# Hybrid RWKV-7 / short-convolution block: the bonus row sums taken by float32 strips and spread by a load, and three kinds of stores requested by GpSimd

## The chip, the cores and the metric

The kernel runs on one core of a Trainium2 chip. The metric is the device time of one execution in microseconds (us). Three executions of the kernel before took 988.72, 988.27 and 989.01 us, median 988.72. The engines are named as in the profile: PE multiplies matrices (PEld is its weight load), DVE is the vector engine, ACT the scalar engine, POOL is GpSimd, and SP requests most of the transfers (DMAs).

## What is computed

One layer. A normalised input of 528 tokens (16 meta tokens and 512 real ones) by 2048 features is multiplied by one large matrix; half of its columns feed 16 recurrent heads of 64 channels, the other half a short convolution; both are gated, joined and multiplied by an output matrix. The change touches the bonus term of the recurrent heads, a sum over the 64 channels of a head, and the gate.

```python
P = hn @ w_in[l]
...
r, k, v, g_r = ...          # 1024 columns each, after the token shift
...
y = _rwkv7_recurrence(rh, decay, kh, vh, kk, kk * ah)
...
bonus = jnp.sum(rh * kh * r_k[l], axis=-1, keepdims=True) * vh
y_a = (yn + bonus.reshape(bsz, L, D_RWKV)) * jax.nn.silu(g_r)
...
mix = jnp.concatenate([y_a, y_b], axis=-1)
h_res = h_res + mix @ w_out[l]
```

## The kernel before

**Tiling.** Channels lie on the 128 partitions and tokens along the free axis. The recurrent heads are worked in 8 pairs, each 128 channels. The input product is a list of column tiles (lora, then k, r, v for the pairs, g for two pairs at a time, and the convolution's C, h, B and gc). A tile is 96 matmuls in two banks, or 48 in one, in four quarters of the contraction. Each weight is kept in two parts: `wr` holds 128x1024 raw float32 values, loaded by SP (line 159, three buffers); for each half, ACT makes the high part (line 151) and DVE the low part (line 152) in a `w` tile (six buffers). The products of a tile go to `ps_k`, `ps_C` and so on (lines 353 and 368).

**Two streams in one.** The function `mains` is a generator of those tiles. `prepare(i)` writes out the work of pair i and calls `fill(ns)` in between, which issues main matmuls worth that many nanoseconds by a counter kept in the program. `later(ns, fn)` puts an action off until that counter has gone on by ns. PE's instructions stand in the order in which they are written; those of the other engines are placed by a scheduler, and each engine works through its own list in order. `tc.issue_after(...)` keeps an instruction behind a named one.

**The pair's work.** `r` (128x512) is multiplied by the per-channel factor and by the key (line 735). In `gram_meta` a pair's squared keys `sq` are summed over each head's 64 channels by four float32 matmuls with a 128x32 block of `cs` (line 788, `key_norms`), each with 144 of the tokens and each writing another strip of 32 partitions of a bank that the next main tile is to use; ACT copies the sums to `n2`. For the bonus, `r` is split into a high and a low part (`rk_h` by ACT, line 665; `rk_l` by DVE, line 666), and two matmuls with a 128x128 block matrix `ones` (lines 820 and 821) write each head's sum into all 64 rows of the other head, in the bank `zb`; ACT copies that over `r` (line 822), DVE multiplies by `v` (line 920, called r times v here), and SP stores the product to `rbd[i]` for the end of the kernel. The value tiles are laid out with the heads swapped, which is why a head's sum goes to the other head's rows. After that come 16x16 triangular inverses on 72 partitions: a chain of small DVE operations (`prod`, `tt`, `y`, lines 874 to 889), which starts when the norms `nd` and blocks `d` have come back from memory.

**Single buffers.** `v` and `g` have one buffer each: the next `v` tile waits until r times v is done, and the second `g` of two waits until the first has been stored to `gated[i]` (line 473). The gate is formed by `g<-pr_g` (line 432) and `g<-th_r,g` (line 442) on DVE. Evacuations of C and h are `u<-ps_C` and `hh<-ps_h` (line 404), with a few columns mended by POOL from `ex` (line 407).

Of the kernel before, what the change touches and what calls it, by code (L numbers as in the profile page):

```python
# [9 lines left out]
F32 = mybir.dt.float32  # L10
F32R = mybir.dt.float32r
I32 = mybir.dt.int32
AF = mybir.ActivationFunctionType
ALU = mybir.AluOpType
# [4 lines left out]
P = 128  # L19
DM = 2048  # L20
KT = DM // P
SEQ = 512
META = 16
L = SEQ + META
CH = 64
NCH = SEQ // CH + 1
LP = NCH * CH
# [5 lines left out]
C_ID, C_GM, C_BM, C_ON = 0, 128, 384, 512  # L33
# [9 lines left out]
FW = dict(  # L43
    evac=34, start=1062, lora=2200, gram=8800, meta={0: 2000}, gram_b=13500, gram2=5500, misc=2000, v=2000, vt=1000, solve=24500, more={0: 5500, 2: 2400},
    tr=3200, lev=3000, cp=4200, out=1500, begin=19500, p=2900, u=2900, s=4200, mid=1000, last=3700, mix=2600,
)
# [43 lines left out]
def hymba_kernel(ctx: ExitStack, tc: tile.TileContext, xt, xtok, front, w_in, w_out, pv, lup, cst, msk, gf, out):  # L90
    nc = tc.nc
    ctx.enter_context(tc.manual_schedule(engines={mybir.EngineType.PE}))
    cp = ctx.enter_context(tc.tile_pool(name="cp", bufs=1))
    dp = ctx.enter_context(tc.tile_pool(name="dp", bufs=2, space=DRAM))
# [3 lines left out]
    cs = cp.tile([P, C_N], F32, name="cs")  # L98
# [6 lines left out]
    rbd = [dp.tile([P, SEQ], F32, tag=f"rbd{j}", name=f"rbd{j}", bufs=1) for j in range(NPAIR)]  # L105
    gated = [dp.tile([P, SEQ], F32, tag=f"gated{j}", name=f"gated{j}", bufs=1) for j in range(NPAIR)]
# [26 lines left out]
    quarters, chain, low = {}, {}, {}  # L133
# [35 lines left out]
    xp = ph1.enter_context(tc.tile_pool(name="xp", bufs=1))  # L169
# [3 lines left out]
    rst = xp.tile([P, 4], F32, name="rst")  # L173
    rsx = cq.tile([P, 2 * META], F32, name="rsx")
    la = cq.tile([P, 2, L], F32R, name="la")
    ones = xp.tile([P, P], F32R, name="ones")
    omm = xp.tile([P, 33], F32, name="omm")
    hv = xp.tile([P, 6, 8], F32, name="hv")
    hl = cp.tile([P, 2, 8], F32, name="hl")
# [3 lines left out]
    pi = ph1.enter_context(tc.tile_pool(name="pi", bufs=1, space=PSUM))  # L183
# [5 lines left out]
    def tr(name, dt=F32):  # L189
        return cq.tile([P, LP], dt, tag="tr", name=name, bufs=5)  # L190
# [122 lines left out]
    with tc.issue_after(head):  # L313
        nc.vector.tensor_scalar(
            out=omm, in0=pvt[:, V_MU : V_MU + 33], scalar1=-1.0, scalar2=1.0, op0=ALU.mult, op1=ALU.add
        )
        for d, off in (
# [4 lines left out]
                out=d, in0=pvt[:, off : off + 8], scalar1=0.5, scalar2=None, op0=ALU.mult  # L322
# [2 lines left out]
            out=hv[:, 4], in0=pvt[:, V_KA : V_KA + 8], scalar1=-0.5, scalar2=1.0, op0=ALU.mult, op1=ALU.add  # L325
        )

    nc.scalar.copy(ones, cs[:, C_BM : C_BM + P])
    FULL = ((0, 272), (272, L))
    TAIL = ((14, 272), (272, L))  # L330
    REAL = ((META, L),)
# [128 lines left out]
    def use(what, i, ps):  # L460
        if what == "lora":
            use_lora(ps)
        elif what in ("k", "v"):
            t = cq.tile([P, LP], F32, tag=what, name=f"{what}{i}")
            nc.gpsimd.memset(t[:, META:CH], 0.0)
            shift_full(ps, tile_of[what] + i, f"{what}{i}", padded(t))
            got[what, i] = t
        elif what in ("r", "g"):
            t = cq.tile([P, SEQ], F32, tag=f"r{i % 2}" if what == "r" else "g", name=f"{what}{i}")
            shift_real(ps, tile_of[what] + i, f"{what}{i}", t)  # L470
            if what == "g":
                gate(t, f"r{i}")
                later(14000, lambda: nc.sync.dma_start(gated[i], t))
            got[what, i] = t
        elif what == "C":
            u = tm(f"u{i}")
            scaled(TAIL, ps, u, 14)
            got[what, i] = u
        elif what == "h":
            u = got["C", i]  # L480
            hh = tm(f"hh{i}")
            with behind_of("turned"):
                scaled(TAIL, ps, hh, 14)
            n = SEQ + 2
            nc.gpsimd.tensor_tensor(out=u[:, 0:n], in0=u[:, 0:n], in1=hh[:, 0:n], op=ALU.mult)
            cv = tp.tile([P, SEQ], F32, tag="cw", name=f"cv{i}")
            nc.scalar.activation(cv, u[:, 0:SEQ], AF.Copy, scale=col(V_CW, i))
            for j in (1, 2):
                with behind_of("conv"):
                    nc.vector.scalar_tensor_tensor(  # L490
                        out=cv, in0=u[:, j : j + SEQ], scalar=col(V_CW, 8 * j + i), in1=cv, op0=ALU.mult, op1=ALU.add
                    )
            got[what, i] = cv
            if i == 0:
                nc.gpsimd.tensor_tensor(out=cv, in0=cv, in1=got["B", 0], op=ALU.mult)
        elif what == "B":
            b = tm(f"b{i}")[:, 0:SEQ] if i else tp.tile([P, SEQ], F32, name="b0")
            scaled(REAL, ps, b, META)
            got[what, i] = b
            if i:  # L500
                nc.gpsimd.tensor_tensor(out=got["h", i], in0=got["h", i], in1=b, op=ALU.mult)
        else:
            cv = got["h", i]
            g = tm(f"gc{i}")[:, 0:SEQ]
            with behind_of("split"):
                scaled(REAL, ps, g, META)
            gate(g, f"c{i}")
            o = direct.get(8 + i, cv)
            nc.vector.scalar_tensor_tensor(out=o, in0=cv, scalar=0.5, in1=g, op0=ALU.mult, op1=ALU.mult)
            if o is cv:  # L510
                later(9000, lambda: nc.sync.dma_start(mixd[8 + i], cv))
        ready.add((what, i))

    ready = set()
# [81 lines left out]
    def later(ns, fn):  # L596
        pending.append((clock[0] + ns, fn))
        pending.sort(key=lambda e: e[0])
# [16 lines left out]
    def fill(ns):  # L615
        while ns > 0:
            seen = len(ready)
            t = step()
            if t is None:
                return  # L620
            ns -= t
            if len(ready) > seen:
                ns += FW["evac"]
# [35 lines left out]
        nc.vector.tensor_tensor(out=lo, in0=raw, in1=hi.bitcast(F32), op=ALU.subtract)  # L659
        return hi, lo  # L660

    def split(t, name, n):
        hi = tr(f"{name}_h", F32R)[:, 0:n]
        lo = tr(f"{name}_l", F32R)[:, 0:n]
        nc.scalar.copy(hi, t)
        nc.vector.tensor_tensor(out=lo, in0=t, in1=hi.bitcast(F32), op=ALU.subtract)
        return hi, lo

    heads = [(h, slice(64 * h, 64 * h + 64), slice(64 - 64 * h, 128 - 64 * h)) for h in range(2)]

    place = [(i % 2) * 4 + i // 2 for i in range(NPAIR)]
# [11 lines left out]
    def behind(dst, src):  # L683
        with tc.issue_after(state["dma"]):
            nc.sync.dma_start(dst, src)
# [8 lines left out]
    def prepare(i):  # L694
        p = i % 2
# [35 lines left out]
        r = got["r", i]  # L731
# [6 lines left out]

        sq = tr(f"sq{i}")
        nc.scalar.activation(sq, k, AF.Square, scale=col(V_KK, i))  # L740
        rh, rl = split(r, f"rk{i}", SEQ)
        fill(FW["gram_b" if p else "gram"] + FW["meta"].get(i, 0))

        late = state["step"] > 48
# [16 lines left out]

        def gram_meta():
            z = early or next_banks()
            norms = key_norms(z[0][:, 96 : 96 + NS]) if late else None
            for h, hs, ho in heads:
                nc.tensor.matmul(
                    z[h][:, 0:META],
                    bk[hs, 0, h : h + 2, :].rearrange("p a s -> p (a s)"),
                    ar[hs, 0, 0, 0:META],
                    start=True, stop=True,  # L770
                )
            norms = norms if late else key_norms(z[0][:, 96 : 96 + NS])
            if p and "levels" in state:
                state["out"] = state.pop("levels").pop(0)(second_level(z))
            with ahead():
                for h in range(2):
                    nc.vector.tensor_tensor(
                        out=gt[:, h, 0, 0:META], in0=z[h][:, 0:META], in1=gmask[:, h, 0:META], op=ALU.mult
                    )
            with ahead():  # L780
                nc.scalar.copy(n2, norms)
            if "out" in state:
                state.pop("out")()
            state["banks"] = z

        def key_norms(z):
            for j in range(4):
                nc.tensor.matmul(
                    z[32 * j : 32 * j + 32], cs[:, C_BM + 48 : C_BM + 80], sq[:, j * NS : (j + 1) * NS],
                    start=True, stop=True, tile_position=(0, 32 * j),  # L790
                )
            return z
# [11 lines left out]

        NS = LP // 4
        n2 = tr(f"n2{i}")[:, 0:NS]
        if late:
            gram_meta()
        za = [pz.tile([P, 4, P], F32, tag="tz", name=f"g{i}_1_{h}") for h in range(2)]
# [4 lines left out]
            gram_meta()  # L814
        masked(za, 1, 5)
        masked(zc, 5, 9)
        fill(FW["gram2"] - FW["meta"].get(i, 0))

        zb = pi.tile([P, SEQ], F32, tag="ser", name=f"zb{i}")
        nc.tensor.matmul(zb, ones[:, 0:P], rh, start=True, stop=False)  # L820
        nc.tensor.matmul(zb, ones[:, 0:P], rl, start=False, stop=True)
        nc.scalar.copy(r, zb)
        fill(FW["misc"])


        bt = cq.tile([P, 2, NCH - 1, CH], F32, tag="bt", name=f"bt{i}")
        for a in range(2):
# [23 lines left out]
        nd = cq.tile([NB, 16], F32, tag="nd", name=f"nd{i}")  # L851
        behind(d, blocks(sg))
        behind(nd, sn.rearrange("(p s) -> p s", s=16))
        y = cq.tile([NB, 256], F32, tag="y", name=f"y{i}").rearrange("p (s t) -> p s t", t=16)
        nc.gpsimd.memset(y, 0.0)
        nc.vector.tensor_scalar(out=nd, in0=nd, scalar1=1e-24, scalar2=None, op0=ALU.max)
# [60 lines left out]
                    ))  # L917
        until("v", i)
        v = got["v", i]
        nc.vector.tensor_tensor(out=r, in0=r, in1=v[:, CH:LP], op=ALU.mult)  # L920
        later(12500, lambda: nc.sync.dma_start(rbd[i], r))
        fill(FW["v"])

        vs = cq.tile([P, NCH, CH], F32, tag="vs", name=f"vs{i}")
# [793 lines left out]
```

## Time and profile before

| | |
|---|---|
| time of three executions | 988.72, 988.27, 989.01 us |
| the profiled execution | 987.58 us, of which its span 985.8 us |
| granted PE clock, mean over the span | 0.998 |
| idle time of ACT before line 665, waiting for line 735 | 14.2 us, 7 times |
| POOL waiting to clear the next v, for r times v | 45.8 us, 7 times |
| SP waiting for a raw weight buffer (line 159, on line 152) | 239.9 us, 60 times |
| data moved | 174.74 MB, 213864 packets |

The span runs from the first to the last instruction; the time of an execution has 1.8 us more around it. A row of a wait names the waiting engine and line, what it waited for, the sum, the number of times and the longest.

### The profile page before, as it was taken

To read this page: it belongs to the slowest core of one execution; us is meant where nothing else is said; L and a number is where in the kernel's file an instruction comes from. 1 tells how busy PE (TensorE), PEld (TensorE's weight loads), DVE (VectorE), ACT (ScalarE), POOL (GpSimd) and SP (SyncE) were. 2 spreads that over 40 slices of the span, in tenths; PEclk is the share of its full clock that TensorE was granted. 3 is DMA by queue.
4 is the path that set the end of the run, shared out by engine and by line. 5 is a ranking of instruction groups with operands and counts; after the bars stand their busy time and mean duration, and the time that the engine had idled before them with its cause. 6 is when DMAs were issued, how large, how long until landed. Compare 5 with 4: busy or idle time off the path is not lost.

```text
span 985.8 us, 22369 instructions
## 1 busy us (share of the span) xinstructions
PE 976.5 (99%) x8999; PEld 906.3 (92%) x8999; DVE 708.3 (72%) x1423; ACT 401.0 (41%) x746; POOL 122.5 (12%) x241
## 2 busy tenths in 40 slices
PE   9999999999999999999999999999999999999996
PEld 9999999999998999998999998989899898888885
DVE  6787956578675678664678665455655799997897
ACT  7653323344322434322533322333343426556454
POOL 0120201112010111010110010010212102001001
PEclk9999999999999999999999999999999999999999
DMA  9526677256576285863285865997876799797654
GB/s 316 169 89 149 147 190 182 81 137 154 133 172 182 91 189 125 201 162 98 87 186 126 194 164 169 281 260 183 232 199 167 199 275 255 190 322 177 158 127 171
DMA packets 213864, 174.74 MB, mean 177 GB/s; under 512 B 157120, under 2 KB 177408, under 8 KB 213376
## 3 DMA queue, kind: packets, MB, share of 16 engines
q1 hardware_dynamic: 211312, 164.66, 61.2%
q0 software_dynamic: 2304, 8.39, 4.9%
q8 instruction: 70, 1.15, 0.5%
q14 instruction: 34, 0.28, 0.1%
q10 hardware_dynamic: 144, 0.26, 0.1%
HBM read 136.92 MB, written 36.35 MB: 176 GB/s over the span
## 4 chain that ended last, share of the span: by engine, by line
PE 93%; DVE 4%; issue 1%; DMA 1%; ACT 0%; POOL 0%; POOLq 0%; DVEq 0%; ACTq 0%
PE ps_v L353 9%; PE ps_C L353 9%; PE ps_g L353 9%; PE ps_gc L368 9%; PE ps_B L368 9%; PE ps_k L353 8%; PE ps_h L353 8%; PE ps_r L353 8%; PE M L1409 7%; PE P L1409 3%; PE g L755 2%; PE Q L1409 1%; PE ps_k L368 1%; PE ps_r L368 1%; PE ps_lora L368 1%
## 5 line engine op out<-in xcount | busy, mean ns | idle before, releaser
L152 DVE TENSOR_TENSOR w<-wr,w 128x512 fp32r<-128x512 f32 x252 | 174.9, 707 | 109.9 <-ACT w L151 104.0
L151 ACT CAST w<-wr 128x512 fp32r<-128x512 f32 x252 | 153.1, 619 | 246.9 <-PE ps_k L353 39.0
L353 PE MATMUL ps_v<-xh,w 128*128 128x256 f32 (+2 forms) x512 | 84.0, 284 | 0.0
L368 PE MATMUL ps_B<-xh,w 128*128 128x512 f32 x256 | 83.4, 394 | 0.3 <-DVE w L152 0.3
L353 PE MATMUL ps_h<-xh,w 128*128 128x256 f32 (+2 forms) x512 | 81.7, 281 | 0.0
L353 PE MATMUL ps_g<-xh,w 128*128 128x256 f32 (+2 forms) x512 | 81.4, 281 | 0.0
L368 PE MATMUL ps_gc<-xh,w 128*128 128x512 f32 x256 | 81.0, 392 | 0.0
L353 PE MATMUL ps_C<-xh,w 128*128 128x256 f32 (+2 forms) x512 | 80.8, 281 | 0.0
L353 PEld LDWEIGHTS ps_v<-xh,w 128*128 128x128 f32 x512 | 73.9, 188 | 0.3
L353 PE MATMUL ps_k<-xh,w 128*128 128x256 f32 (+1 forms) x448 | 73.3, 285 | 0.0
L353 PE MATMUL ps_r<-xh,w 128*128 128x256 f32 (+1 forms) x448 | 72.6, 281 | 0.0
L353 PEld LDWEIGHTS ps_g<-xh,w 128*128 128x128 f32 x512 | 71.9, 189 | 0.6 <-issue 0.2
L353 PEld LDWEIGHTS ps_h<-xh,w 128*128 128x128 f32 x512 | 72.1, 189 | 0.3
L353 PEld LDWEIGHTS ps_C<-xh,w 128*128 128x128 f32 x512 | 71.7, 189 | 0.2
L353 PEld LDWEIGHTS ps_k<-xh,w 128*128 128x128 f32 x448 | 64.7, 188 | 0.4
L353 PEld LDWEIGHTS ps_r<-xh,w 128*128 128x128 f32 x448 | 63.5, 189 | 0.4 <-issue 0.2
L368 PEld LDWEIGHTS ps_B<-xh,w 128*128 128x128 f32 x256 | 47.8, 188 | 10.3 <-DVE w L152 0.7
L368 PEld LDWEIGHTS ps_gc<-xh,w 128*128 128x128 f32 x256 | 47.7, 188 | 10.1
L353 PE MATMUL ps_h<-xl,w 128*128 128x256 f32 x256 | 56.7, 280 | 0.0
L353 PE MATMUL ps_C<-xl,w 128*128 128x256 f32 x256 | 55.9, 279 | 0.0
L353 PE MATMUL ps_v<-xl,w 128*128 128x256 f32 x256 | 55.8, 278 | 0.0
L353 PE MATMUL ps_g<-xl,w 128*128 128x256 f32 x256 | 55.4, 278 | 0.0
(384 smaller groups left out, 2085.2 us busy)
## 6 DMA issues: line engine op xcount, KB each, us to landing
wr<-in_w_in_dram SPq DMA_DIRECT2D x126, 512.0 KB
ct<-opd SPq DMA_DIRECT2D x72, 192.0 KB
wo<-in_w_out_dram SPq DMA_DIRECT2D x24, 512.0 KB
x<-in_w_out_dram POOLq DMA_DIRECT2D x16, 512.0 KB, 5.6
opd<-gt SPq DMA_DIRECT2D x16, 288.0 KB
bd<-bt SPq DMA_DIRECT2D x64, 64.0 KB
bw<-bd SPq DMA_DIRECT2D x16, 256.0 KB
x<-in_w_out_dram SPq DMA_DIRECT2D x8, 512.0 KB
```

Of the source, the lines that this page charges most:

```text
L151: nc.scalar.copy(hi, rq)
L152: low[q] = eng.tensor_tensor(out=lo, in0=rq, in1=hi.bitcast(F32), op=ALU.subtract).ins
L353: nc.tensor.matmul(ps[r][:, 0 : b - a], ww[:, k * P : (k + 1) * P], xx[:, kt, a:b], start=(kt == 0 and n == 0), stop=(kt == KT - 1 and n = ...
L368: nc.tensor.matmul(ps[r], ww[:, w], xx[:, kt, a:b], start=(kt == 0 and n == 0), stop=(kt == KT - 1 and n == 2))
L755: nc.tensor.matmul(z[h][:, c - c0], bk[hs, c, h : h + 2, :].rearrange("p a s -> p (a s)"), ar[hs, c].rearrange("p a s -> p (a s)"), start= ...
L1409: nc.tensor.matmul(bank[s], left(prod, jj, m, s), w, start=(jj == 0 and n == 0), stop=(jj == 7 and n == 2))
```

## The change

The bonus sums are now taken in `gram_meta`, beside the key norms and in the same way: four float32 matmuls of 128 tokens each, from `r` itself, into four strips of the second bank. ACT copies them to `nb`. POOL stores `nb` as 1024 values in memory (`sb`, two DMAs), and SP loads them back into `r`, each head's 512 sums into 64 partitions (`spread`). The split of `r`, the `zb` matmuls, the copy and the matrix `ones` go. r times v is put off by 9.5 to 12 us of the counter, and its store by 12 us more; that store and the gate's stores (put off by 20 us instead of 14) are requested by POOL.

```diff
-    nc.scalar.copy(ones, cs[:, C_BM : C_BM + P])
...
-                later(14000, lambda: nc.sync.dma_start(gated[i], t))
+                later(20000, lambda: nc.gpsimd.dma_start(gated[i], t))
...
-        rh, rl = split(r, f"rk{i}", SEQ)
...
             with ahead():
                 nc.scalar.copy(n2, norms)
+                nc.scalar.copy(nb, bonus)
...
-        def key_norms(z):
+        def sums_of(z):
+            return head_sums(z[0][:, 96 : 96 + NS], sq, NS), head_sums(z[1][:, 96 : 96 + P], r, P)
+
+        def head_sums(z, x, n):
             for j in range(4):
                 nc.tensor.matmul(
-                    z[32 * j : 32 * j + 32], cs[:, C_BM + 48 : C_BM + 80], sq[:, j * NS : (j + 1) * NS],
+                    z[32 * j : 32 * j + 32], cs[:, C_BM + 48 : C_BM + 80], x[:, j * n : (j + 1) * n],
                     start=True, stop=True, tile_position=(0, 32 * j),
                 )
             return z
...
-        zb = pi.tile([P, SEQ], F32, tag="ser", name=f"zb{i}")
-        nc.tensor.matmul(zb, ones[:, 0:P], rh, start=True, stop=False)
-        nc.tensor.matmul(zb, ones[:, 0:P], rl, start=False, stop=True)
-        nc.scalar.copy(r, zb)
-        fill(FW["misc"])
...
+        sb = dp.tile([2 * SEQ], F32, tag="sb", name=f"sb{i}")
+
+        def put_sums():
+            for h in range(2):
+                nc.gpsimd.dma_start(sb[h * SEQ : (h + 1) * SEQ].rearrange("(j s) -> j s", s=P), nb[16 * h : P : 32])
+
+        spread = bass.AP(tensor=sb.tensor, offset=sb.offset, ap=[[SEQ, 2], [0, CH], [1, SEQ]])
+        later(1000, put_sums)
+        later(5000, lambda: nc.sync.dma_start(r, spread))
...
-        nc.vector.tensor_tensor(out=r, in0=r, in1=v[:, CH:LP], op=ALU.mult)
-        later(12500, lambda: nc.sync.dma_start(rbd[i], r))
+
+        def bonus_rows():
+            assert ("v", i + 1) not in ready
+            with tc.issue_after(low[max(low)]):
+                nc.vector.tensor_tensor(out=r, in0=r, in1=v[:, CH:LP], op=ALU.mult)
+
+        wait = 12000 if p else 9500 if i else 10500
+        later(wait, bonus_rows)
+        later(wait + 12000, lambda: nc.gpsimd.dma_start(rbd[i], r))
```

What stands where is shown for pair 3 (the fourth). On PE, before: the key norms at the end of the pair's products, and further on the two bonus matmuls among main matmuls (`g_5_1` is a product of the pair, `sq` the squared keys, `ps_g` a main tile).

```order
L755 MATMUL g_5_1_3501<-ar_3120,bk_3121 128x128
L766 MATMUL ps_C_0_3518<-ar_3120,bk_3121 128x16
L766 MATMUL ps_C_1_3519<-ar_3120,bk_3121 128x16
L788 MATMUL ps_C_0_3518<-sq_3300,cs 32x144 x4
...
L353 MATMUL ps_g_0_3488<-xl,w_3347 128x256
L820 MATMUL zb_3635<-rk_h,ones 128x512
L821 MATMUL zb_3635<-rk_l,ones 128x512
L353 MATMUL ps_g_0_3488<-xh,w_3347 128x256 x2
```

And now:

```order
L745 MATMUL g_5_1_3500<-ar_3120,bk_3121 128x128
L757 MATMUL ps_C_0_3517<-ar_3120,bk_3121 128x16
L757 MATMUL ps_C_1_3518<-ar_3120,bk_3121 128x16
L784 MATMUL ps_C_0_3517<-sq_3301,cs 32x144 x4
L784 MATMUL ps_C_1_3518<-r_3157,cs 32x128 x4
```

Four strips from `r` follow the four from `sq`, and the `zb` pair is gone; main matmuls move by one to three places around such spots.

On DVE, around the inverse of pair 3, the rows before, from the first step after the norms to the last half of `hh` (`w_3755` and `w_3758` are low parts of weights; the small steps left out are the same in both):

```order
L862 COPY y_3675<-nd_3672 72x16
L152 TENSOR_TENSOR w_3755<-wr_3753,w_3755 128x512
L152 TENSOR_TENSOR w_3758<-wr_3753,w_3758 128x512
...
L403 TENSOR_TENSOR ex<-ps_C_1_3519,rst 128x4
...
L432 SCALAR_TENSOR_TENSOR g_3740<-pr_g_3741,omm,sh_g_3747 128x512
L880 TENSOR_REDUCE tt_3680<-prod_3679 72x64
L404 TENSOR_TENSOR u_3878<-ps_C_0_3518,rs 128x256
L404 TENSOR_TENSOR u_3878<-ps_C_1_3519,rs 128x256
L883 TENSOR_TENSOR prod_3679<-y_3675,tt_3680 72x512
L442 SCALAR_TENSOR_TENSOR g_3740<-th_r_3750,g_3740 128x512
```

And the rows there now:

```order
L430 SCALAR_TENSOR_TENSOR g_3745<-pr_g_3746,omm,sh_g_3752 128x512
L440 SCALAR_TENSOR_TENSOR g_3745<-th_r_3755,g_3745 128x512
...
L402 TENSOR_TENSOR u_3883<-ps_C_0_3517,rs 128x256
...
L401 TENSOR_TENSOR ex<-ps_C_1_3518,rst 128x4
L402 TENSOR_TENSOR u_3883<-ps_C_1_3518,rs 128x256
...
L152 TENSOR_TENSOR w_3760<-wr_3758,w_3760 128x512
L152 TENSOR_TENSOR w_3763<-wr_3758,w_3763 128x512
...
L879 TENSOR_REDUCE tt_3680<-prod_3679 72x16
L923 TENSOR_TENSOR r_3157<-r_3157,v_3331 128x512
L882 TENSOR_TENSOR prod_3679<-y_3675,tt_3680 72x64
```

The two gate operations and the first half of `u` have moved ahead of `ex`, which needs the finished tile `ps_C`; two weight splits have moved behind it, and r times v into the inverse.

On SP, the requests now around the spreading load of the same pair:

```order
L676 DMA nd_3671<-sn_3665 72x16
L672 DMA opd_73<-ar_3120 64x9x64
L676 DMA d_3670<-sg_3664 72x16x16
L159 DMA wr_3758<-in_w_in_dram 128x1024
L672 DMA opd_73<-ar_3120 64x9x64
L852 DMA r_3157<-sb_3674 128x1x512
L159 DMA wr_3792<-in_w_in_dram 128x1024
```

The load `r<-sb` stands directly ahead of the request of the weights `wr_3792`; before, the other rows stood there without it.

More of the change, by code (lines that the diff above doesn't have):

```diff
@@ L175, in hymba_kernel @@
     la = cq.tile([P, 2, L], F32R, name="la")
-    ones = xp.tile([P, P], F32R, name="ones")
     omm = xp.tile([P, 33], F32, name="omm")
@@ L660, in lora_up @@
         return hi, lo
[L662 to L667, printed above, removed]
     heads = [(h, slice(64 * h, 64 * h + 64), slice(64 - 64 * h, 128 - 64 * h)) for h in range(2)]
@@ L763, in gram_meta @@
             z = early or next_banks()
-            norms = key_norms(z[0][:, 96 : 96 + NS]) if late else None
+            if late:
+                norms, bonus = sums_of(z)
             for h, hs, ho in heads:
@@ L771, in gram_meta @@
                 )
-            norms = norms if late else key_norms(z[0][:, 96 : 96 + NS])
+            if not late:
+                norms, bonus = sums_of(z)
             if p and "levels" in state:
@@ L806, in prepare @@
         n2 = tr(f"n2{i}")[:, 0:NS]
+        nb = tr(f"nb{i}")[:, 0:P]
         if late:
@@ L816, in prepare @@
         masked(zc, 5, 9)
-        fill(FW["gram2"] - FW["meta"].get(i, 0))
-        zb = pi.tile([P, SEQ], F32, tag="ser", name=f"zb{i}")
-        nc.tensor.matmul(zb, ones[:, 0:P], rh, start=True, stop=False)
-        nc.tensor.matmul(zb, ones[:, 0:P], rl, start=False, stop=True)
-        nc.scalar.copy(r, zb)
-        fill(FW["misc"])
+        fill(FW["gram2"] - FW["meta"].get(i, 0) + FW["misc"])
         bt = cq.tile([P, 2, NCH - 1, CH], F32, tag="bt", name=f"bt{i}")
```

## The prediction

> **What bounds the kernel now.** First the page: the engines' shares, then the chain of waits by engine, then the idle time that ended last on PE.
>
> ```profile
> span 985.8 us, 22369 instructions
> ...
> PE 976.5 (99%) x8999; PEld 906.3 (92%) x8999; DVE 708.3 (72%) x1423; ACT 401.0 (41%) x746; POOL 122.5 (12%) x241
> ...
> PE 93%; DVE 4%; issue 1%; DMA 1%; ACT 0%; POOL 0%; POOLq 0%; DVEq 0%; ACTq 0%
> ...
> PE ps_B L368 <- DVE w L152: 0.3, 1, 0.3
> PEld ps_B L368 <- DVE w L152: 0.7, 1, 0.7
> ```
>
> PE is busy for 976.5 of 985.8 us, and PE rows carry 93% of the chain. Apart from the start-up, the page names one wait of PE, a short stop in the main part. So the kernel is bound by what PE executes: an instruction taken off PE is worth its full time, and work on other engines counts only where it makes PE wait. To find that place I followed the chain through the 60 us around the stop.
>
> ```profile
> 253.09 0.38 PE ps_C L788 x8
> ...
> 260.21 0.23 PE zb L820
> 260.44 0.23 PE zb L821
> ...
> 265.46 11.19 PE ps_C L353 x96
> ...
> 276.90 0.62 DVE xn L949
> ...
> 281.63 1.28 DVE w L152 x2
> ...
> 284.69 0.66 DVE g L432
> ...
> 285.95 0.66 DVE u L404 x2
> ...
> 287.67 0.20 DVE g L442
> 287.87 0.32 issue
> ...
> 289.27 0.34 DVE hh L404
> ...
> 289.74 1.31 POOL u L485
> ...
> 293.29 0.69 DVE w L152
> ...
> 294.03 4.64 PE ps_B L368 x19
> ```
>
> Columns are start, length, engine, written tile, line, count. PE leads up to 265.46 + 11.19 = 276.65. Then the inverse of pair 3 and what is queued among its steps fill DVE up to 289.61 without a gap; a hand-over through POOL and ACT follows, and the low part of a weight is ready at 293.98, just too late for the matmul of 294.03. **This stretch is the one place where a microsecond more or less on DVE reaches PE.**
>
> **PE, the sum.** Removed per pair are the two `zb` matmuls, 0.23 + 0.23 = 0.46 us on the chain, eight times 3.7 us. Added is a second group of strips. The key norms are the same instructions with 144 instead of 128 columns, and take 0.38 us. By columns the new group takes 0.38 x 128/144 = 0.34 us. Bounds: no column saved gives 0.38. From the other side:
>
> ```profile
> 391.69 0.30 PE L766 MATMUL ps_g<-ar,bk 64*128 64x16 f32 x4
> 391.92 0.45 PE L788 MATMUL ps_g<-sq,cs 128*32 128x144 f32 x8
> ```
>
> Four 16-column matmul records in float32 occupy 391.92 - 391.69 = 0.23 us, the nearest row for short strips; I hold 0.23 as the least. So a pair saves 0.46 - 0.34 = 0.12 us (0.08 to 0.23), and the kernel **0.96 us** (0.64 to 1.84). I take 0.34, since row 788 is the same instruction at nearly this size.
>
> A strip group now needs `r` as line 735 leaves it. The tightest pair is pair 4:
>
> ```profile
> 343.23 0.70 DVE L735 SCALAR_TENSOR_TENSOR r<-r,hv,ta 128x512 f32<-128x512 f32 x1
> 346.51 0.45 PE L788 MATMUL ps_k<-sq,cs 128*32 128x144 f32 x8
> ```
>
> The product ends at 343.93, the strips come at 346.51 + 0.38 = 346.89: 3.0 us to spare, so no new wait. If the cover went, each microsecond would be one of PE.
>
> **ACT and DVE outside the stretch.** Removed per pair are the split of `r`, a cast and a subtraction (least, median and longest in ns):
>
> ```profile
> L665 ACT CAST rk_h<-r x8: 604/622/622, 75.9 to 529.3; 128x512 fp32r<-128x512 f32 x8
> L666 DVE TENSOR_TENSOR rk_l<-r,rk_h x8: 651/684/693, 77.7 to 530.3; 128x512 fp32r<-128x512 f32 x8
> ```
>
> The copy of `zb` goes too; its successor, the copy into `nb`, has a quarter of its columns, so ACT gains 0.62 us and more a pair, and DVE 0.68 us. ACT at 41% and DVE at 72% are not what PE waits for there, so I count nothing. Freed DVE time elsewhere has no wait of PE to shorten.
>
> **DVE in the stretch.** The order rows show what goes in and out. Out, ahead of the steps that need the finished `ps_C`: the gate operations, with 0.66 us (line 432) and 0.20 + 0.32 (line 442), half of the two `u` (0.33), and `xn` (0.62), which now stands ahead of `ex` and need not wait for the second bank: 2.13 us. In: two low parts of weights (1.28) and r times v:
>
> ```profile
> 261.38 0.69 DVE L920 TENSOR_TENSOR r<-r,v 128x512 f32<-128x512 f32 x1 [0.55 <-ACT r L822]
> 270.72 0.69 DVE L152 TENSOR_TENSOR w<-wr,w 128x512 fp32r<-128x512 f32 x1 [2.61 <-ACT w L151]
> ```
>
> Together 1.97 us. The gate operations can go early because `g` has one buffer: its earlier store was requested late on SP, now POOL requests it. 1.97 - 2.13 = -0.16 us is within what such a replay can tell, and I take **nothing**. Bounds: what comes in counts in full and nothing leaves, +1.97; the stop vanishes, -0.7 by its PEld row. The moved low parts were made at 270.72; now they come some 6 us later, at about 278. They belong to the third quarter of the tile after `ps_C`; at 11.19 us a tile that is 276.65 + 5.6 = 282.2, so four microseconds cover them. If `xn` or `u` could not go early, 0.95 us would come back, and PE would stop longer by it, one to one.
>
> **Transfers.** Each pair gets three new ones: two stores of `nb` and the spreading load. A trip to memory and back of this small kind is already there:
>
> ```profile
> 211.29 1.11 SPq L685 DMA_DIRECT2D sn<-n  x2
> ...
> 214.35 0.34 SPq L685 DMA_DIRECT2D nd<-sn  x1
> ```
>
> The request of `nd`, which waits for `sn`, goes out about 2 us after the last store is issued. The load fills 128x512 float32, 0.262 MB, and its first question is how many of the 16 DMA engines it has.
>
> ```profile
> q1 hardware_dynamic: 211312, 164.66, 61.2%
> ...
> 269.79 0.64 SPq L159 DMA_DIRECT2D wr<-in_w_in_dram  x1
> ```
>
> The queue moved 164.66 MB in 0.612 x 16 x 985.8 us of engine time: 17.1 KB per us and engine. As an estimate the load takes 1.0 us on 16 engines, and 262/17.1 = 15.4 us on one. In pair 3 it is requested at about 269, before the weights of 269.79. r times v is reached near 283: it stands one small step behind the pair of splits that ends on the chain at 281.63 + 1.28 = 282.91, and about as much has left the steps ahead of it as has come in. `r` must have landed by then, 14 us after the request. The load needs 1 to 15.4 us by these bounds, and some 2 us of a trip; I take the short end, since the nearest row, the queue that moves the weights, spreads its work over the 16 engines at 61% each in the mean; so the load is hidden. The Trainium skill, in "DMA: Bandwidth & Descriptors", section "Rules for kernel authors", says that an outermost dimension smaller than 16 confines a transfer to that many engines; the load's source begins with 2. No row of this trace shows such a load. By that rule the load is estimated at 7.7 us and lands near 279, with 4 us to spare instead of 11: the sum stays, the late-load rival below comes nearer. No run here shows it so far.
>
> POOL's requests cost POOL, not PE:
>
> ```profile
> L1360 POOL DMA_DIRECT2D x<-in_w_out_dram x16: 858/871/1101, 821.9 to 950.5; - x16
> ```
>
> Four more per pair at most (two sums, product, gate) at 0.87 us are 28 us in all; POOL is 12% busy. What hides them is its idle time, and the price appears only where a mend of columns (as `u L485` at 289.74) waits behind one: at most 0.87 us. SP is relieved of as many requests (0.64 us for one on the row above) and gets eight loads; as the page names no wait of PE for a transfer or for POOL, I count nothing (bounds: 0 and the 0.87 us).
>
> **Sum.** -0.96 + 0 = -0.96. The profiled execution is its span of 985.8 plus 1.8, 987.6; changed, 986.6. The median of the three executions stands 1.1 higher, and 988.72 - 0.96 = 987.76: **987.8 us**. A measurement of this kernel can tell about 0.2%, which is 1.98 us, so 986.74 to 990.70 is "same". The change would be real and too small to see.
>
> **Rivals.**
>
> *The stretch gets shorter and the strips are cheap.* The added group costs 0.23 us, and the stop of 0.7 us goes: 988.72 - 1.84 - 0.7 = 986.2. For it: `xn`, `u` and `g` leave the stretch. Against: row 788 costs 0.38, not 0.23, and the low parts come in. 0.10, "faster".
>
> *The moved work lengthens the stretch.* +1.97 with the saving: 988.72 - 0.96 + 1.97 = 989.7; with the least saving 990.1. For it: DVE has no gap there. Against: as much leaves as enters. 0.07, "same".
>
> *The spreading load lands late and DVE stands still in the inverse, slower.* One mechanism in pair 3: r times v is in DVE's queue ahead of the later steps, and `hh`, `u`, `cv` and the weight's low part stand behind it, so PE waits for them. It decides from a landing later than 14 us after the request, a transfer of more than 12. With one engine: 269 + 15.4 + 2 (the trip) = 286.4, against 283, 3.4 us late, and the stretch hands it on: 988.72 - 0.96 + 3.4 = 991.2. For it: the weights requested next share the engines (61% busy in the mean). Against: only the top of the span from 1 to 15.4 us is beyond 12, and the low end is the likelier. 0.09, "slower".
>
> *The change does not do what it says:* if the float32 strips cost as much as the pair removed (0.46), the sum is zero and the time 988.7. Against: the key norms' row. 0.04, "same".
>
> The forecast has the remaining **0.70**. Faster 0.10, same 0.70 + 0.07 + 0.04 = 0.81, slower 0.09. The range goes from 986.2 (all low bounds) to 990.1 (least saving and the full stretch); only the late load is outside it, which leaves out less than 2 in 10, and the unknown costs allow no narrower one.
>
> **What would show it.** In the changed profile: second strip group of about 0.34 us behind the key norms on PE and no `zb`; the stop of PE before `ps_B` near 293 at 0 to 1 us; the inverse of pair 3 still without a gap on DVE, r times v without a wait for a DMA; POOL at some 15%. A row of DVE idle for `r<-sb`, or a second wait of PE of more than a microsecond, would make the prediction wrong, and so would a strip group of 0.5 us or more.

## The result, and the profile after

The changed kernel takes **996.64 us** (median of 4 executions, 995.93 to 999.98) against 988.5 us before (4 executions: the three given further up and one of 987.86): a ratio of 1.0089, with a 95% interval of 1.0066 to 1.0113. It is slower by about 8 us, where 987.8 was forecast. The profiled execution has a span of 995.2 us, 9.4 more than before. First the lines of the page that answer to those shown of before: engines, queue of SP, chain by engine, and the waits of PE and of DVE for transfers (us in total, times, longest).

```profile
span 995.2 us, 22529 instructions
...
PE 976.7 (98%) x9047; PEld 906.4 (91%) x9047; DVE 703.5 (71%) x1415; ACT 391.5 (39%) x737; POOL 148.8 (15%) x273
...
q1 hardware_dynamic: 210048, 162.57, 60.1%
...
PE 77%; DMA 9%; DVE 7%; issue 2%; SPq 2%; POOL 1%; ACT 1%; POOLq 0%; DVEq 0%; ACTq 0%
```

```profile
DVE tt L862 <- DMA d<-sg: 11.3, 3, 4.1
PE t L970 <- DVE xn L955: 6.8, 3, 2.8
DVE xn L955 <- DMA xT<-sx: 5.0, 2, 4.3
PE ta L633 <- ACT tz L638: 2.4, 2, 1.3
```

PE is busy about as long as before (976.7 us against 976.5), but its share of the chain has fallen from 93% to 77%, and DMA's has risen from 1% to 9%. PE now stands still in five places that did not exist before, 6.8 + 2.4 = 9.2 us: three in front of the `t` matmuls (at 300.63, 440.55 and 590.82 us), which need `xn`, and two in front of `ta` (at 372.70 and 523.65 us). Each goes back to a transfer. In front of the first and the last `t`, `xn` waits for `xT`. In front of the middle one, with 2.77 us the longest, `xn` stands on DVE behind two low parts of weights, and these weights landed 5.40 us after their request. In front of both `ta` stands a chain that begins at `d`. The chain in front of the first stop, at 300.63 us (start, length, what; SPq is the time that SP takes to make a request):

```profile
290.56 0.45 SPq L934
...
291.62 3.88 DMA sx<-y
...
295.52 0.61 SPq L894
...
296.17 0.64 SPq L895
...
296.85 2.91 DMA xT<-sx
...
299.86 0.72 DVE xn L955
...
300.63 0.67 PE t L970 x32
```

A small transfer of 72 KB takes 3.88 us to land and its successor 2.91, and SP's own requests are links of the chain: `sx` could not be requested before SP was through with what stood ahead of it. So the place to look is SP's list, behind the spreading load. Pair 7, in the timeline of SP, of the kernel before, and then of the changed one (`opd<-gt` are four requests of 144 to 288 KB that follow the load):

```profile
551.75 0.62 SPq L159 DMA_DIRECT2D wr<-in_w_in_dram  x1
552.41 0.59 SPq L681 DMA_DIRECT2D opd<-ar  x1
553.04 4.75 SPq L681 DMA_DIRECT2D opd<-gt  x4
557.84 1.78 SPq L910 DMA_DIRECT2D bd<-bt  x3
559.72 0.45 SPq L159 DMA_DIRECT2D wr<-in_w_in_dram  x1
...
570.75 0.36 SPq L904 DMA_DIRECT2D sx<-y  x1
```

```profile
559.73 0.63 SPq L159 DMA_DIRECT2D wr<-in_w_in_dram  x1
560.40 0.59 SPq L672 DMA_DIRECT2D opd<-ar  x1
561.15 0.56 SPq L852 DMA_DIRECT2D r<-sb  x1
561.76 9.00 SPq L672 DMA_DIRECT2D opd<-gt  x4
570.81 1.78 SPq L909 DMA_DIRECT2D bd<-bt  x3
572.68 0.48 SPq L159 DMA_DIRECT2D wr<-in_w_in_dram  x1
...
581.18 1.45 SPq L903 DMA_DIRECT2D sx<-y  x1
```

The load itself takes SP 0.56 us. The four requests behind it take 9.00 us in place of 4.75, and the next weights are asked for 572.68 - 559.73 = 12.95 us after the last ones, in place of 559.72 - 551.75 = 7.97. Over the whole kernel (least, median and longest of the 32 requests in ns, of before and after):

```profile
L681 SPq DMA_DIRECT2D opd<-gt x32: 580/1161/2784, 90.2 to 556.4; - x32
```

```profile
L672 SPq DMA_DIRECT2D opd<-gt x32: 586/2176/5060, 92.2 to 567.3; - x32
```

The sum of these 32 is 35.2 us before and 64.7 after. The records of the packets show what is particular about the load: its 128 rows of 2 KB move in 5.5 to 6.7 us, with 10.8 to 12.5 us of DMA engine time in all, as much as two engines at work all that time; the records do not name the engines.

In front of `ta` the transfer itself is slow. In pair 4, before, `d` is requested at 353.89 us (by line 685), and DVE has it at 357.41, 3.5 us later:

```profile
357.41 0.16 DVE L863 TENSOR_TENSOR tt<-d,nd 72x8 f32<-72x8 f32 x1 [0.26 <-DMA d<-sg]
```

Now it is requested 1.5 us after the spreading load and takes 8.46 us, though it has 72 KB. The load's own packets end at 362.46, 2.3 us before `d` lands:

```profile
356.29 8.46 DMA d<-sg
...
372.70 0.39 PE ta L633
```

So what is asked for behind the load comes late in two ways: SP gets to its request late (`sx`, and by it `xT`), or the transfer, once requested, lands late (`d`).

### The profile page after: what moved, and what is told of

The parts are those of the page before. It is cut to its first block, busy times and chain, and to the rows that moved or that the text cites. A ratio compares the mean times of both kernels' runs of the same rounds, so it can differ in the third digit from the quotient of the medians.

```text
span 995.2 us, 22529 instructions
## 1 busy us (share of the span) xinstructions
PE 976.7 (98%) x9047; PEld 906.4 (91%) x9047; DVE 703.5 (71%) x1415; ACT 391.5 (39%) x737; POOL 148.8 (15%) x273
## 4 chain that ended last, share of the span: by engine, by line
PE 77%; DMA 9%; DVE 7%; issue 2%; SPq 2%; POOL 1%; ACT 1%; POOLq 0%; DVEq 0%; ACTq 0%
PE ps_gc L366 9%; PE ps_B L366 8%; PE ps_v L351 8%; PE M L1415 7%; PE ps_g L351 7%; PE ps_h L351 6%; PE ps_C L351 6%; PE ps_r L351 6%; PE ps_k L351 5%; PE P L1415 3%; DMA d<-sg 3%; DMA wr<-in_w_in_dram 2%; PE Q L1415 2%; PE ps_k L366 1%; PE ps_r L366 1%
## 5 line engine op out<-in xcount | busy, mean ns | idle before, releaser
L151 ACT CAST w<-wr 128x512 fp32r<-128x512 f32 x252 | 152.0, 618 | 273.0 <-DMA wr<-in_w_in_dram 46.6
```

Of the source, the lines that this page charges most:

```text
L151: nc.scalar.copy(hi, rq)
```

## The experiments

Theory A: the narrow load is what costs, by what stands behind it. The rivals are B (what DVE does later) and C (POOL's requests). Each ratio is to the kernel before in the same session. All kernels compute the whole layer; the loads that e4 and e5 add go to a tile that nothing reads.

**Two loads of 64 rows** (changed kernel, e1). Each load's source now begins with a dimension of 64:

```diff
-        spread = bass.AP(tensor=sb.tensor, offset=sb.offset, ap=[[SEQ, 2], [0, CH], [1, SEQ]])
+            for h in range(2):
+                nc.sync.dma_start(
+                    r[64 * h : 64 * h + 64],
+                    bass.AP(tensor=sb.tensor, offset=sb.offset + h * SEQ, ap=[[0, CH], [1, SEQ]]),
+                )
```

> The changed kernel, with the spreading load written as two loads of 64 rows each, one per head, so that no outermost dimension is 2. Theory A (the load sits on two DMA engines for 6.2 us, SP's next requests get stuck behind it, and everything that SP feeds comes late): the 128 packets of a load end within 2 to 3 us, SP's time for the requests of opd<-gt falls from 64.7 us back to about 35, the five stops of PE (2.1, 1.5, 3.0, 1.3 and 2.4 us at 300 to 591) go, and the time is 986.5 to 988.5 us. Theory B (what DVE does later, r times v and the moved splits, makes PE wait): the stops stay and the time stays near 996. Theory C (POOL's requests hold up POOL's mends): stays near 996.

985.87 us (985.2 to 989.37), ratio 0.998 [0.997, 0.999], a little below the range expected. All five stops are gone; the same bytes move in 1.6 to 3.0 us. Its chain by engine, and pair 7 on SP:

```profile
PE 95%; DVE 2%; DMA 1%; issue 1%; ACT 0%; POOL 0%; POOLq 0%; DVEq 0%; ACTq 0%
```

```profile
551.38 2.04 SPq L852 DMA_DIRECT2D r<-sb  x2
553.46 4.01 SPq L672 DMA_DIRECT2D opd<-gt  x4
```

The requests behind the load are back from 9.00 to 4.01 us, and the kernel is 0.2% faster than before. Theory A holds; B and C, which leave this edit no effect, fall.

**All stores requested by SP** (changed kernel, e2: `nc.gpsimd` to `nc.sync` in the three stores).

> The changed kernel, with all three kinds of stores requested by SP again, at the same places of the program. Theory A: the narrow load is still there and SP has more requests besides; 995 to 999 us. Theory C (POOL): the loss goes, about 988. Theory B: near 996.

1004.39 us, ratio 1.0161 [1.0135, 1.0186]: worse than theory A's range, and the opposite of C. POOL's requests are not the cost; they save something.

**Only the product's and the gate's stores by POOL** (kernel before, e3).

> The kernel before, with only the product's and the gate's stores requested by POOL (the gate's put off by 20 us of the counter, as in the change). Theories A and B: 988 to 989, no difference. Theory C: 992 or more.

986.91 us, ratio 0.9986 [0.9978, 0.9995]. A small gain that none of the theories had; C falls again. The stop of PE at 294 us is gone.

**An additional narrow load** (kernel before, e4), and the **same bytes in two wide loads** (e5):

```diff
+        dm = cq.tile([P, SEQ], F32, tag="dm", name=f"dm{i}")
+        spread = bass.AP(tensor=w_in.tensor, offset=w_in.offset, ap=[[1024, 2], [0, CH], [1, SEQ]])
+        later(5000, lambda: nc.sync.dma_start(dm, spread))
```

> The kernel before, with an additional load per pair, of the shape and at the place of the spreading load (two rows of 2 KB, each into 64 partitions), into a tile that nothing reads; all else as before. Theory A: SP's requests of opd<-gt grow as in the changed kernel, and PE gets stops in pairs 3 to 7; 993 to 998 us. Theories B and C: the load alone costs nothing that is seen, 988 to 989.5.

> The kernel before with the same 256 KB per pair loaded additionally as two loads of 64 rows, into a tile that nothing reads. Theory A (the narrowness costs, not the bytes): 987.5 to 990, PE without stops over 0.6 us. If it were the bytes or one more request in SP's list: as with the narrow extra load, 998 to 1007.

1003.9 us (ratio 1.0156 [1.0135, 1.0177]; 998.62 to 1006.89) and 989.52 us (1.0011 [1.0002, 1.0019]). The narrow load alone, with nothing of the change beside it, costs more than the whole change, and above the range expected; the bytes and one request more cost about 1 us, with two short stops of PE, 0.6 and 1.0 us, of which the second was not expected. In the profiled execution with the narrow load (998.62 us) PE's stops come to 6.7 us, and 3.4 us more go to two stretches at half clock (see the last section). On SP, in pair 7 of the two:

```profile
561.11 0.59 SPq L856 DMA_DIRECT2D dm<-in_w_in_dram  x1
561.74 7.07 SPq L681 DMA_DIRECT2D opd<-gt  x4
```

```profile
553.38 1.28 SPq L858 DMA_DIRECT2D dm<-in_w_in_dram  x2
554.70 3.98 SPq L681 DMA_DIRECT2D opd<-gt  x4
```

**Four and two engines, in two loads** (changed kernel, e7 and e9: the source of each of the two loads is written `[[0, 4], [0, CH // 4], [1, SEQ]]`, and `[[0, 2], [0, CH // 2], [1, SEQ]]`; the same rows, another outermost dimension).

> The changed kernel with two loads of 64 rows, whose source is written with an outermost dimension of 4 (4 times 16 rows) in place of 64. Theory A: each of the two loads sits on four engines, the same four, 128 packets in about 3 us; opd<-gt between 31 and 45 us, stops of PE small or none, 986 to 990. If the shape of the source made no difference: as the two loads of 64, 985.9.

> Two loads of 64 rows each, as in e1_two_loads, but the source of each written with an outermost dimension of 2 (2 times 32 rows). Theory A, with the number of engines set by the outermost dimension: both loads sit on the same two engines, 128 packets take about 6 us again, opd<-gt is at 55 to 70 us, and the time 994 to 1000. If what counts is that one request carries both heads: as the two loads of 64, 985 to 987.

With 4: 986.72 us (0.9986 [0.9978, 0.9995]), packets in 3.1 to 5.2 us, `opd<-gt` at 38.2 us, as expected. With 2: 1000.69 us (1.0133 [1.0113, 1.0153]), just above its range, packets in 5.4 to 7.3 us. So it is the outermost dimension and not the number of requests, and most of the harm sets in between 4 and 2. One expectation missed: with 2, the requests of `opd<-gt` sum to only 46.8 us, below the 55 to 70 expected, while the 126 of `wr` take SP 69.6 us, against 55.3 with two loads of 64; the hold falls on whatever stands behind.

**The narrow load requested by others.** By ACT (changed kernel, e6: `nc.scalar.dma_start(r, spread)`), and by POOL as the two loads of two times 32 rows (e13), with the two wide loads by POOL as control (e14).

> The changed kernel, with the same narrow load requested by ACT in place of SP. Theory A1 (what costs is that SP's own queue is full behind the load, so that SP is held at its next requests): opd<-gt falls from 64.7 us to below 45, the stops of PE become small, 986 to 990 us. Theory A2 (what costs is that two of the 16 engines are taken for 6 us, whoever asked): opd<-gt falls, but weights and xT still land late through those two engines; 990 to 997 us.

> The two loads of two times 32 rows of e9_two_by_two, requested by POOL in place of SP, so that they stand in POOL's queue. Theory A1 (the harm is that SP's own queue is full and SP is held): opd<-gt falls back to a median near 0.65 to 1.2 us, no stop of PE over 1 us, 985.5 to 989. Theory A2 (the harm is that a few DMA engines are taken for some microseconds, whoever asked): stops of PE stay, 991 to 1001.

> The two loads of 64 rows of e1_two_loads, requested by POOL in place of SP: SP has 16 requests fewer. Theory A: as e1_two_loads or a little less, 984.5 to 986.5. If POOL's requests (0.6 to 0.9 us each) now hold up its mends: 987 or more.

1009.72 us (1.0212 [1.0194, 1.023]), 1004.14 us (1.0184 [1.0157, 1.0211]) and 984.96 us (0.9971 [0.996, 0.9982]). The first two are above every range expected; the third is the fastest of all versions. In the kernel with the narrow loads by POOL, SP's `opd<-gt` has a median of 1200 ns, as in its control (1210), and the sums are 46.7 and 40.9 us, so SP is hardly held there; the time is 19 us above the control all the same. That SP alone carries the harm (A1) falls. POOL's timeline in pair 4 of it shows the hold in its new place (in brackets the idle time before, and what ended it):

```profile
356.99 0.70 POOL L852 DMA_DIRECT2D r<-sb  x1 [1.11 <-DVE pr_v L402]
363.88 0.67 POOL L852 DMA_DIRECT2D r<-sb  x1 [6.19 <-DMA d<-sg]
...
364.65 0.21 POOL L405 TENSOR_TENSOR pr_v<-ex 128x2 f32<-128x2 f32 x1
```

POOL stands 6.19 us between the two requests, and its mends of `pr_v` come behind. The row puts the end of that wait down to `d<-sg`, but the first load landed at 363.50, and in all eight pairs the second request goes out 0.35 to 0.38 us after the first load has landed. In the control the second follows at once in five pairs of eight. With ACT's request, ACT's casts of weights waited more for the weights:

```profile
ACT w L151 <- DMA wr<-in_w_in_dram: 72.0, 17, 11.9
```

This was 46.6 us in the changed kernel. SP's `opd<-gt` falls to 46.9 us, nearly as far as theory A1 had it, and the time rises all the same. But ACT also stands still in front of its request, until the stored sums have landed: 26.4 us in seven pairs, up to 5.1 us at once, where SP's waits at that line come to 0.8 us. These are the rows of its sequencer:

```profile
L852 ACTq EVENT_SEMAPHORE  x13: 17/2872/5066, 88.2 to 563.0; - x13
```

No run has the wide loads requested by ACT, so what the narrowness costs there is open. With POOL there is a control: the requester of the narrow loads is hurt, and so are transfers asked for by others (ACT's wait for the weights that SP requests is 48.0 us against 23.5 in the control). How much of the harm is the one and how much the other these runs do not tell, since POOL does other work of PE's chain as well.

**Which store matters** (e8: two wide loads, all stores by SP; e11: the gate's alone by SP; e12: sums' and product's by SP; e10: kernel before with the gate's store alone by POOL).

> Two loads of 64 rows, and all three kinds of stores requested by SP. By the step of 8 us that SP's stores cost beside the narrow load (996.6 to 1004.4), 990 to 994; if that step was only the queue behind the narrow load, 986 to 989 (the product's and gate's stores by POOL alone gave -1.4 us on the kernel before).

> Two loads of 64 rows, the gate's stores alone requested by SP, the others by POOL. If the 12.4 us between the two loads of 64 with POOL's and with SP's stores come from the gate's store (a gate operation on DVE waits for it, and u stands behind it): 995 to 1000, with stops of PE near 154 and 296. If not: 985.5 to 988.

> Two loads of 64 rows, the stores of the sums and of the product requested by SP, the gate's by POOL. By the gate's store as the cause: 985.5 to 988. If these two kinds of stores are the cause: 993 to 1000.

> The kernel before, with only the gate's stores requested by POOL (put off by 20 us of the counter). If the gain of 1.4 us of the two kinds of stores by POOL comes from the gate operations that leave the inverse of pair 3: 986.5 to 987.5, and the stop of PE at 294 is gone. If it comes from the product's stores: 988 to 988.8, and the stop stays.

998.29 us (1.01 [1.0072, 1.0128]), 991.78 (1.0049 [1.003, 1.0067]), 988.73 (1.0009 [1.0, 1.0018]), 987.46 (0.9994 [0.9985, 1.0002]). The first is above both its ranges, the second and the third lie between theirs. The fourth lies in the first of its ranges and its profile has no stop at 294, as expected of the gate operations, but its time cannot be told from no change. The gate's store is about half of the 12.4 us that lie between e1 and all stores by SP, and the sums' and the product's are about 3 us. The rest is about what the clock took in the profiled execution of e8: two stretches at half clock, in which PE worked 5.75 and 3.40 us, so 4.6 us lost, while the profile of e11 has none; the six executions of e8 lie between 993.54 and 1002.41. With all stores by SP, two waits are named in the main part, and DVE's timeline in pair 3 shows the reason:

```profile
PE ps_gc L366 <- DVE u L402: 3.0, 1, 3.0
PE ps_B L366 <- DVE u L402: 2.9, 1, 2.9
```

```profile
292.86 0.68 DVE L894 TENSOR_REDUCE y<-prod 72x64 f32<-72x512 f32 x1
293.46 1.28 DVE L152 TENSOR_TENSOR w<-wr,w 128x512 fp32r<-128x512 f32 x2
294.66 0.68 DVE L929 TENSOR_TENSOR r<-r,v 128x512 f32<-128x512 f32 x1
...
295.33 0.74 DVE L430 SCALAR_TENSOR_TENSOR g<-pr_g,omm,sh_g 128x512 f32<-128x512 f32 x1
296.00 0.74 DVE L402 TENSOR_TENSOR u<-ps_C,rs 128x256 f32<-128x256 f32 x2
```

With the store late on SP, the gate operation is placed behind the inverse, `u` behind it, and the banks of `ps_C` come free only then: the stretch that the prediction named, now lengthened. In e8 and e11 the gate's store stays put off by 20 us of the counter; in the kernel before, SP requests it at 14 us and PE's stop there is 0.3 us. No run has SP's request at 14 us beside the wide loads, so whether the requester or the later moment costs is open.

## Why the prediction was wrong

**The step that failed** is the one on transfers: "so the load is hidden", with "I count nothing (bounds: 0 and the 0.87 us)" for SP's and POOL's requests. The load itself was taken at the short end, 1.0 us of transfer, and its packets took 5.5 to 6.7; that alone cost nothing. The load was weighed by one question only, whether it lands before r times v. That was answered rightly: in pair 3 it is requested at 271.62, its last packet ends at 280.15, and r times v starts at 283.83; r times v had no idle time before it in any pair.

```profile
L923 DVE TENSOR_TENSOR r<-r,v 128x512 f32<-128x512 f32 x8 | 5.4, 680 | 0.0
```

The rule of the Trainium skill that was cited there ("DMA: Bandwidth & Descriptors", "Rules for kernel authors") agrees with the trace: two engines, 5.5 to 6.7 us of packets where 7.7 was the estimate. What the prediction did not ask is what stands in the queue *behind* a transfer that keeps two engines for six microseconds, and what those requests feed. Behind it stood `opd`, `bd`, two loads of weights and the inverse's way through memory, `sx` and `xT`, and in the pairs 2, 4 and 6 also `d`; they had little time to spare: DVE waited 2.0 us for `d` before, and 11.3 after, in these three pairs. Nothing was counted because the page named no wait of PE for a transfer; but a page without such waits only says that the slack was enough so far, not how large it is.

**The sum against the trace.** The span grew by 9.4 us. The changed kernel and e1 have the same PE instructions in the same order, so their starts can be set side by side: over the five stops the changed kernel falls back by 2.0, 1.6, 3.0, 1.4 and 2.3 us, 10.4 with unrounded figures, and by another 1.2 in small steps, 0.5 of it at 252 us and 0.3 at the start. e1's span is 2.2 us shorter than that of the kernel before, as much as the strips (1.9) and the stop in front of `ps_B` that is gone (0.3) make. So -2.2 + 10.4 + 1.2 = 9.4. The sum's own terms:

*PE's strips:* right in kind, mis-sized. The two groups of the changed kernel, and what follows them:

```profile
253.12 0.45 PE L784 MATMUL ps_C<-sq,cs 128*32 128x144 f32 x8
253.39 0.40 PE L784 MATMUL ps_C<-r,cs 128*32 128x128 f32 x8
253.72 0.22 PE L1032 MATMUL ps_C<-xT,tm 32*32 32x32 f32 x2
```

Both take 253.72 - 253.12 = 0.60 us, where one took 0.38: the second costs 0.22, not 0.34, and a pair saves 0.46 - 0.22 = 0.24 us, eight times 1.9 in place of 0.96. It lies at the low end, 0.23, that the prediction had drawn from the short strips.

*The stretch of pair 3:* counted at nothing, and about that. PE's named wait in front of `ps_B`, 0.3 us before, is in neither the changed kernel's rows of waits nor in those with the wide loads. The gate's stores by POOL keep it so at that moment of the counter, as e8 and e11 show: there PE stops for 2.9 and 1.7 us in front of `ps_B`, the kind of loss that the +1.97 bound stood for.

*POOL's requests:* at 15% busy as forecast, and no stop of PE for them in e1, which has them all.

*The rivals.* The slower rival named the load but another way to PE: DVE standing still at r times v, which did not happen. Its point of decision, a transfer of more than 12 us, was drawn from that way; a transfer of 6 us was enough by the other. With the load spread over more engines the rest of the change comes out as the faster rival had it: 986.2 was worked out for cheap strips and no stop, and 985.87 was measured.

## What to carry to other kernels

A load that spreads a few rows over the partitions by a zero step should have the large dimension outermost: the same 256 KB took 5.5 to 6.7 us with a dimension of 2 outermost and 1.6 to 3.0 us with 64, and the kernel's time went from 996.6 to 985.9. Ask of a new transfer not only when it lands, but what is behind it, in its queue and on its DMA engines, and how much time those had to spare; that must be read from the waits of the other engines, since PE's own are empty until the slack is used up. A store that frees a single buffer should not come late: with the gate's store requested by POOL, DVE's gate operations left a full stretch; with the same store by SP, at the same moment of the counter, they stood in it, and the time was 5.9 us longer.

## What the runs showed of the hardware

A stop of PE can cost more than its length. In the kernel with the narrow load and all stores by SP (e2), the granted clock fell to half after four stops of PE, of 1.9 to 2.8 us: for 3.4 us after three of them, for 6.8 after the last. Two further stops, of 1.7 and 1.8 us, were not followed by one. Around the first of the four (columns as in the view of windows: busy time and count of PE, PEld, DVE, ACT and POOL, then the granted clock, the DMA share and GB/s):

```profile
150.00:153.50 3.50, 1.62 (x14) 1.42 (x13) 3.46 (x7) 0.39 (x1) 0.19 (x1) 1.00 1.09 256
153.70:157.10 3.40, 3.40 (x9) 2.62 (x10) 1.30 (x4) 0.96 (x3) 1.60 (x1) 0.51 0.69 113
157.30:160.00 2.70, 2.70 (x13) 2.23 (x12) 2.53 (x4) 1.67 (x4) 0.00 (x0) 1.00 0.81 211
```

Half a clock for 3.4 us is 1.7 us lost. In the kernel with the additional narrow load (e4), stops of 2.4 and 2.7 us were each followed by 3.4 us at half clock. In the profiled execution of the changed kernel no such stretch followed, though its longest stop was 2.8 us too; another execution of it, at a mean clock of 0.993 in place of 0.999, took 999.98 us. So like stops cost a different amount from one execution to the next, which would fit the wide ranges of the kernels with stops (998.62 to 1006.89 for the extra narrow load) beside 984.86 to 986.07 for the fastest kernel.
